# Weight halves of 4 bytes in turns in one tile, and every moving operand 128 bytes modulo 256 away

## The chip, the cores and the metric

The kernel runs on one core of one Trainium2 chip. The metric is the device time of one execution in microseconds. Five engines work side by side: TensorE (PE in the profile, its weight loads are PEld), VectorE (DVE), ScalarE (ACT), GpSimd (POOL) and SyncE (SP), which here only starts the DMAs.

## The reference

Two blocks of two layers each over 256 positions of width 1024, all in float32. Each layer is a mixer and a feed-forward net around a residual stream:

```python
x = x + ssd_mixer(rmsnorm(x), ...)        # state-space mixer, 32 heads
x = x + conv_ffn(rmsnorm(x), ...)         # up 1024 -> 5632, conv, silu(g)*u, down 2816 -> 1024
x = x + diff_attention(rmsnorm(x), ...)
x = x + conv_ffn(rmsnorm(x), ...)
# second block: four half-weighted swiglu nets of the same size, a conv mixer with
# attention to a memory, a forgetting attention with attention to a memory, a last rmsnorm
```

Nearly all of the arithmetic is in products of an activation (256 rows) with a weight matrix that is used once: 308.8 MB are read from HBM.

## The kernel before

**Three products for one.** TensorE takes float32 at full pace only as `F32R`, a float32 with fewer mantissa bits. So each operand is split into an upper part (rounded to `F32R`) and a lower part (the rest), and `mm3` adds three products: upper weight by upper activation (L212), upper weight by lower activation (L213), lower weight by upper activation (L214). Each of the three has a weight load of its own, which runs beside the matmul in front of it.

**Weights.** SP loads raw weights into `wr` (three buffers of 2048 floats). `split` takes 1024 columns of it (512 to 768 in some places): ScalarE writes the upper part to the tile `wh` (L202), VectorE subtracts it from the raw weights and writes the lower part to the tile `wl` (L206; in the first stage every fourth goes to GpSimd). Both tiles have five buffers of 4096 bytes a partition, so TensorE can be several pieces behind.

**Activations.** They stand transposed, 128 features by 256 positions, in tiles `xx` (a normed input, made by ScalarE L399 and VectorE L400), `gg` (a feed-forward's inner product) and `yy` (a mixer's output). In each, the upper part of a feature block is followed by its lower part, 1024 bytes each.

**Two forms of product.** In `lin_T` and `lin_out` (through `tile_T`, `tile_out` and `mm3`) 128 columns of the weights are the stationary operand and 256 columns of the activation move. `lin_T` makes projections with 8 blocks of features a tile; `lin_out` makes the eight tiles that go back to the residual stream. In `lin_N` (L285 to L287) it is the other way round: 128 positions of the activation are stationary and 512 columns of the weights move. It makes what is wanted untransposed: z of the state-space mixer (4 calls), query, key and value of the differential attention (6), the memory's values (2) and the forgetting attention's values (2), 14 calls of 48 matmuls each.

**Where the tiles lie.** `Net.t` rounds every tile's size up to `LINE` = 64 bytes. The pools follow each other in SBUF in the order in which they are opened. `wr`, `wh` and `wl` start at multiples of 256 bytes. Behind them L71 puts a tile "apart" of 64 bytes that nothing uses, so that all that follows is shifted by 64. In the built program the moving operands then start, modulo 256: `xx` at 64 in eleven cases and at 192 in three, `gg` at 192 in all six, `yy` at 64 in one and at 192 in three. Since every row of `xx`, `gg` and `yy` has 1024 bytes and every weight block 512, each matmul of a stage has the same distance modulo 256 between its moving operand and the weights that are loaded beside it.

**Order.** The code is written out in the order of the stages; `Net.spawn` and `adv` weave the small work of norms and attention heads into the stream of matmuls, and the tile framework sets the waits. A stage's stream is: load, split by ScalarE and VectorE, 24 matmuls for each split of 1024 columns.

Of the kernel before, what the change touches and what calls it, by code (L numbers as in the profile page):

```python
# [10 lines left out]
F32 = mybir.dt.float32  # L11
F32R = mybir.dt.float32r
# [11 lines left out]
LINE = 64  # L24
# [34 lines left out]
class Net:  # L59
    def __init__(self, ctx, tc, I, out):  # L60
        self.ctx, self.tc, self.nc, self.I, self.out = ctx, tc, tc.nc, I, out
        self.uid = 0
        nc = self.nc
        ps = bass.MemoryType.PSUM
        pool = lambda name, bufs, **k: ctx.enter_context(tc.tile_pool(name=name, bufs=bufs, **k))
        self.const = pool("const", 1)
        self.wr = pool("wr", 3)
        self.wh = pool("wh", 5)
        self.xp = pool("xp", 1)

        self.t(self.xp, [128, LINE // 4], F32, "apart")  # L71
        self.sm = pool("sm", 4)
        self.s2 = pool("s2", 2)
        self.psA = pool("psA", 3, space=ps)
        self.psM = pool("psM", 3, space=ps)
        self.psY = pool("psY", 2, space=ps)
        self.deferred = []
        self.hold = 1
        self.norm = None
        self.now = 0.0  # L80
        self.active = []
        self.waiting = []
        self.cnt = 0
        self.share = 0

        c = self.const
        self.X = self.t(c, [128, KD, S], F32, "X")
        self.cv = self.t(c, [128, NCOL], F32, "cv")
        self.mhalf = self.t(c, [128, 8], F32, "mhalf")
        nc.vector.memset(self.mhalf, -0.5)  # L90
        warm = self.t(c, [128, 8], F32, "warm")
        nc.scalar.activation(out=warm, in_=self.mhalf, func=AF.Silu)

        wz = self.t(self.s2, [128, S], F32, "dg").bitcast(BF16)
        nc.vector.memset(wz, 1.0)
        wp = self.psum(self.psM, "psM")
        for _ in range(11):
            nc.tensor.matmul(wp, lhsT=wz[:, 0:128], rhs=wz, start=True, stop=True)
        nc.sync.dma_start(out=self.cv[:, 0:8], in_=I["cv"][:, 0:8])
        self.first = self.t(self.wr, [128, 2048], F32, "wr")  # L100
        self.second = self.t(self.wr, [128, 2048], F32, "wr")
        for i in range(2):
            c0 = i * 512
            nc.sync.dma_start(out=self.first[:, c0:c0 + 512], in_=I["w_ssd"][0][:, c0:c0 + 512])
            for k in (4 * i, 4 * i + 2):
                nc.sync.dma_start(out=self.X[:, k:k + 2], in_=I["xT"][:, k:k + 2])
        for i in range(2):
            h = slice(i * 1024, i * 1024 + 1024)
            nc.sync.dma_start(out=self.second[:, h], in_=I["w_z"][0, 0][:, h])
        self.third = self.t(self.wr, [128, 2048], F32, "wr")  # L110
        nc.sync.dma_start(out=self.third, in_=I["w_z"][0, 1])
        nc.sync.dma_start(out=self.cv[:, 8:], in_=I["cv"][:, 8:])
        self.rv = self.t(c, [128, NROW], F32, "rv")
        nc.sync.dma_start(out=self.rv, in_=I["rv"].to_broadcast([128, NROW]))
        self.ident = self.t(c, [128, 128], F32, "ident")
        make_identity(nc, self.ident)
        self.identb = self.t(c, [128, 128], BF16, "identb")
        nc.vector.tensor_copy(out=self.identb, in_=self.ident)

        self.sel = self.t(c, [64, 32], F32R, "sel")  # L120
        for p in (0, 32):
            nc.vector.tensor_copy(out=self.sel[p:p + 32], in_=self.ident[p:p + 32, p:p + 32])
        self.ones = self.t(c, [128, 128], F32, "ones")
        nc.vector.memset(self.ones, 1.0)
        self.onesr = self.t(c, [128, 128], F32R, "onesr")
        nc.vector.tensor_copy(out=self.onesr, in_=self.ones)
# [70 lines left out]

    def split(self, raw, c0, n):
        nc = self.nc
        hi = self.t(self.wh, [128, 1024], F32R, "wh")  # L200
        lo = self.t(self.wh, [128, 1024], F32R, "wl")
        nc.scalar.activation(out=hi[:, :n], in_=raw[:, c0:c0 + n], func=AF.Copy)  # L202
        self.cnt += 1
        pool = self.share and self.cnt % self.share == 0 and (self.norm is None or self.norm.done)
        eng = nc.gpsimd if pool else nc.vector
        eng.tensor_tensor(out=lo[:, :n], in0=raw[:, c0:c0 + n],  # L206
                          in1=hi[:, :n].bitcast(F32), op=ALU.subtract)
        return hi, lo
# [120 lines left out]
    def make_norm(self, gname, split=True, sq="act", pool=None):  # L329
        return Norm(self, gname, split, sq, self.xp if pool is None else pool)  # L330
# [30 lines left out]
class Norm:  # L361
    def __init__(self, net, gname, split, sq, pool):
        self.n, self.g, self.split = net, gname, split
        self.done = False
        self.sq = sq
        self.keep = None
        self.wait = 4.5
        self.acc = net.t(net.s2, [128, S], F32, "nacc")
        if split:
            self.xx = net.t(pool, [128, KD, 2, S], F32R, "xx")  # L370
            self.xh, self.xl = self.xx[:, :, 0], self.xx[:, :, 1]
# [86 lines left out]
def first_norm(net, gname):  # L458
    nm = net.make_norm(gname)
    for k in range(KD):  # L460
        nm.scale(k, net.X[:, k])

    def squares():
        for k in range(KD):
            nm.add(k, net.X[:, k])
            if k % 2:
                yield 1

    nm.wait = 5.5
    net.spawn(squares(), 3)  # L470
    return nm


def next_norm(net, gname, split=True, pool=None):
    box = {}

    def after(m):
        if m == 0:
            box["n"] = net.make_norm(gname, split=split, pool=pool)
        box["n"].step(m)  # L480
    return box, after
# [866 lines left out]
def program(ctx, tc, I, out):  # L1348
    net = Net(ctx, tc, I, out)
    nc = net.nc  # L1350
    nm = first_norm(net, "nm0")
    box, after = next_norm(net, "nf0")
    ssd(net, nm, after)
    kvp = ctx.enter_context(tc.tile_pool(name="kvp", bufs=1))
    mk = net.t(kvp, [128, 4, S], F32, "mk")
    mv = net.t(kvp, [128, 2, 512], F32, "mv")
    tables = attn_tables(net, kvp)
    b2, after = next_norm(net, "nm1")
    ffn(net, box["n"], I["up0"], I["dn0"], 1.0, 0, after)
    b3, after = next_norm(net, "nf1")  # L1360
    diff_attn(net, b2["n"], mk, mv, kvp, tables, after)
    b4, after = next_norm(net, "f00")
    ffn(net, b3["n"], I["up1"], I["dn1"], 1.0, 1, after)
    b5, after = next_norm(net, "mx0")
    ffn(net, b4["n"], I["up2"], I["dn2"], 0.5, None, after)
    b6, after = next_norm(net, "f01")
    mixer_a(net, b5["n"], mk, mv, after)
    kvp = ctx.enter_context(tc.tile_pool(name="kvf", bufs=1))
    kT = net.t(kvp, [128, 8, S], F32, "kT")
    vN = net.t(kvp, [128, 2, D], F32, "vN")  # L1370
    cc2 = net.t(kvp, [64, S], F32R, "cc2")
    cN = net.t(kvp, [128, 2, 32], F32, "cN")
    cx = ExitStack()
    kvx = cx.enter_context(tc.tile_pool(name="kvx", bufs=1))
    b7, after = next_norm(net, "kvn", pool=kvx)
    ffn(net, b6["n"], I["up3"], I["dn3"], 0.5, None, after)
    n8 = kvf(net, b7["n"], "f10", kT, vN, cc2, cN)
    cx.close()
    b9, after = next_norm(net, "mx1")
    ffn(net, n8, I["up4"], I["dn4"], 0.5, None, after)  # L1380
    b10, after = next_norm(net, "f11")
    mixer_b(net, b9["n"], mk, mv, kT, vN, cc2, cN, after)
    b11, after = next_norm(net, "fin", split=False)
    fo = []

    def last(m):
        if m == 0:
            fo.append(net.t(net.xp, [128, 2 * KD, S], F32, "xx"))
        after(m)
        nc.scalar.activation(out=fo[0][:, m], in_=net.X[:, m], func=AF.Copy,  # L1390
                             scale=net.col("fin", m))

    ffn(net, b10["n"], I["up5"], I["dn5"], 0.5, None, last)
    fn = b11["n"]
    fn.force()
    fo = fo[0]
    for k in (0, 2, 1, 3, 4, 6, 5, 7):
        if k in (2, 6):
            nc.gpsimd.tensor_tensor(out=fo[:, k], in0=fo[:, k], in1=fn.R, op=ALU.mult)
        else:  # L1400
            nc.vector.tensor_tensor(out=fo[:, k], in0=fn.ps[:, :S], in1=fo[:, k], op=ALU.mult)
    for k in (0, 2, 4, 6):
        nc.sync.dma_start(out=out[:, k:k + 2], in_=fo[:, k:k + 2])
# [103 lines left out]
```

## Time and profile before

| what | value |
|---|---|
| time, median of 3 runs | 1809.99 us (1808.48 to 1810.47) |
| the profiled execution | 1804.52 us, of which the span of instructions is 1802.8 us |
| TensorE busy | 1768.8 us (98%) |
| VectorE, ScalarE, GpSimd busy | 1237.0 us (69%), 1016.0 us (56%), 490.2 us (27%) |
| granted clock of TensorE, mean | 0.995 |
| HBM traffic | 172 GB/s over the span |

A busy time is the sum of an engine's instructions. Matmuls are pipelined, so the bar of one (0.28 us) is longer than the distance to the next; the pace of TensorE is read from the distance of starts, or from how many bars touch a window of known length: (window + one bar) / count.

### The profile page before, as it was taken

To read this page: it belongs to the slowest core of one execution; us is meant where nothing else is said; L and a number is where in the kernel's file an instruction comes from. 1 tells how busy PE (TensorE), PEld (TensorE's weight loads), DVE (VectorE), ACT (ScalarE), POOL (GpSimd) and SP (SyncE) were. 2 spreads that over 40 slices of the span, in tenths; PEclk is the share of its full clock that TensorE was granted. 3 is DMA by queue.
4 is the path that set the end of the run, shared out by engine and by line. 5 is a ranking of instruction groups with operands and counts; after the bars stand their busy time and mean duration, and the time that the engine had idled before them with its cause. 6 is when DMAs were issued, how large, how long until landed. Compare 5 with 4: busy or idle time off the path is not lost.

```text
span 1802.8 us, 34773 instructions
## 1 busy us (share of the span) xinstructions
PE 1768.8 (98%) x14067; PEld 1702.7 (94%) x14067; DVE 1237.0 (69%) x1863; ACT 1016.0 (56%) x1661; POOL 490.2 (27%) x453
## 2 busy tenths in 40 slices
PE   8889999999999999999999999999999999999997
PEld 7787999998789999999999999999999998999997
DVE  6998789867786997655567775556655567575554
ACT  7666576656666765554455464455454455464443
POOL 3555224412211442133201214320033210024321
PEclk9999999999999999999999999999999999999999
DMA  6342645455326555655564475545555464265553
GB/s 234 117 141 71 210 169 194 164 178 189 137 89 229 180 188 158 212 187 187 162 216 161 140 235 181 186 155 193 210 187 187 154 221 164 73 231 180 187 161 106
DMA packets 76497, 312.12 MB, mean 173 GB/s; under 512 B 6192, under 2 KB 6320, under 8 KB 72624
## 3 DMA queue, kind: packets, MB, share of 16 engines
q1 hardware_dynamic: 76304, 309.89, 50.5%
q8 instruction: 111, 1.82, 0.4%
q14 instruction: 50, 0.41, 0.1%
q0 software_dynamic: 32, 0.00, 0.0%
HBM read 308.82 MB, written 1.05 MB: 172 GB/s over the span
## 4 chain that ended last, share of the span: by engine, by line
PE 87%; DVE 6%; ACT 2%; DMA 1%; POOL 1%; issue 1%; DVEq 0%; ACTq 0%; POOLq 0%
PE psA L214 25%; PE psA L213 25%; PE psA L212 25%; PE psA L285 2%; PE psA L287 2%; PE psA L286 2%; DVE cvy L848 2%; DVE wl L206 1%; POOL rs L342 1%; PE psM L992 1%; ACT wh L202 1%; DMA wr<-up 0%; PE psY L1137 0%; PE psM L1106 0%; DMA wr<-memT 0%
## 5 line engine op out<-in xcount | busy, mean ns | idle before, releaser
L206 DVE TENSOR_TENSOR wl<-wr,wh 128x1024 fp32r<-128x1024 f32 (+3 forms) x651 | 719.9, 1109 | 382.0 <-ACT wh L202 373.2
L202 ACT ACTIVATE wh<-wr 128x1024 fp32r<-128x1024 f32 (+3 forms) x660 | 629.2, 956 | 493.8 <-PE psA L213 312.4
L214 PE MATMUL psA<-xx,wl 128*128 128x256 f32 x2752 | 771.6, 280 | 4.6 <-DVE wl L206 4.6
L212 PE MATMUL psA<-xx,wh 128*128 128x256 f32 x2752 | 775.4, 282 | 0.4 <-DVE pad L352 0.4
L213 PE MATMUL psA<-xx,wh 128*128 128x256 f32 x2752 | 771.2, 280 | 0.0
L214 PEld LDWEIGHTS psA<-xx,wl 128*128 128x128 f32 x2752 | 517.4, 188 | 6.3 <-DVE wl L206 5.7
L212 PEld LDWEIGHTS psA<-xx,wh 128*128 128x128 f32 x2752 | 517.7, 188 | 2.1 <-PE psA L214 0.6
L213 PEld LDWEIGHTS psA<-xx,wh 128*128 128x128 f32 x2752 | 518.4, 188 | 0.9 <-issue 0.5
L213 PE MATMUL psA<-gg,wh 128*128 128x256 f32 x1056 | 294.1, 279 | 0.0
L214 PE MATMUL psA<-gg,wl 128*128 128x256 f32 x1056 | 294.1, 279 | 0.0
L212 PE MATMUL psA<-gg,wh 128*128 128x256 f32 x1056 | 294.1, 279 | 0.0
L503 POOL TENSOR_TENSOR p<-s,t 128x256 f32<-128x256 f32 x132 | 183.6, 1391 | 368.6 <-ACT s L531 368.6
L214 PEld LDWEIGHTS psA<-gg,wl 128*128 128x128 f32 x1056 | 200.5, 190 | 0.0
L213 PEld LDWEIGHTS psA<-gg,wh 128*128 128x128 f32 x1056 | 198.2, 188 | 0.0
L212 PEld LDWEIGHTS psA<-gg,wh 128*128 128x128 f32 x1056 | 198.2, 188 | 0.0
L390 POOL TENSOR_TENSOR nacc<-nacc,sq 128x256 f32<-128x256 f32 x72 | 63.6, 883 | 479.6 <-ACT sq L334 478.8
L506 POOL TENSOR_TENSOR gg<-p,gg 128x256 fp32r<-128x256 f32 x132 | 109.4, 830 | 125.7 <-ACT gg L505 125.7
L505 ACT ACTIVATE gg<-p 128x256 fp32r<-128x256 f32 x132 | 54.2, 412 | 126.7 <-POOL p L503 126.6
L212 PE MATMUL psA<-yy,wh 128*128 128x256 f32 x384 | 107.8, 282 | 0.2 <-ACT yy L1181 0.2
L213 PE MATMUL psA<-yy,wh 128*128 128x256 f32 x384 | 106.8, 279 | 0.3 <-DVE yy L1182 0.3
L214 PE MATMUL psA<-yy,wl 128*128 128x256 f32 x384 | 106.6, 278 | 0.0
L352 DVE TENSOR_TENSOR t<-psA,R 128x512 f32<-128x512 f32 (+1 forms) x104 | 69.3, 670 | 37.1 <-PE psA L214 35.5
(291 smaller groups left out, 1920.0 us busy)
## 6 DMA issues: line engine op xcount, KB each, us to landing
wr<-up SPq DMA_DIRECT2D x132, 1024.0 KB, 4.8
wr<-dn SPq DMA_DIRECT2D x96, 704.0 KB, 4.0
wr<-w_a SPq DMA_DIRECT2D x14, 1024.0 KB, 4.8
wr<-w_ssd SPq DMA_DIRECT2D x12, 1024.0 KB, 5.0
wr<-w_ain SPq DMA_DIRECT2D x12, 1024.0 KB, 4.8
wr<-w_ssdo SPq DMA_DIRECT2D x16, 512.0 KB, 4.5
wr<-w_z SPq DMA_DIRECT2D x7, 1024.0 KB, 4.8
wr<-w_ao SPq DMA_DIRECT2D x16, 384.0 KB, 3.1
```

What stands on the lines that cost most here:

```text
L202: nc.scalar.activation(out=hi[:, :n], in_=raw[:, c0:c0 + n], func=AF.Copy)
L206: eng.tensor_tensor(out=lo[:, :n], in0=raw[:, c0:c0 + n], in1=hi[:, :n].bitcast(F32), op=ALU.subtract)
L212: mm(ps, lhsT=wh, rhs=xh, start=first, stop=False)
L213: mm(ps, lhsT=wh, rhs=xl, start=False, stop=False)
L214: mm(ps, lhsT=wl, rhs=xh, start=False, stop=last)
L285: mm(ps[b], lhsT=xh[:, k, xs], rhs=hi[:, c], start=k == 0, stop=False)
L286: mm(ps[b], lhsT=xl[:, k, xs], rhs=hi[:, c], start=False, stop=False)
L352: self.nc.vector.tensor_tensor(out=o, in0=p, in1=self.bc(R, n), op=ALU.mult)
L390: eng.tensor_tensor(out=self.acc, in0=self.acc, in1=sq, op=ALU.add)
L503: nc.gpsimd.tensor_tensor(out=p, in0=s, in1=t[:, 1], op=ALU.mult)
L505: nc.scalar.activation(out=gh[:, j], in_=p, func=AF.Copy)
L506: nc.gpsimd.tensor_tensor(out=gl[:, j], in0=p, in1=gh[:, j].bitcast(F32), op=ALU.subtract)
```

## The change

Upper and lower weight parts now share one tile `w` of 128 x 1024 x 2 floats under the tag `wh`: the upper part is `w[:, :, 0]`, the lower `w[:, :, 1]`. ScalarE and VectorE write every second float, VectorE also reads the upper part with that step, weight loads of L212 to L214 read 128 floats at a step of 8 bytes (1024 bytes of address in place of 512), and in `lin_N` the moving operand is 512 floats at a step of 8 bytes. The unused tile behind the weights grows from 64 to 128 bytes, and a second one of 128 bytes stands at the start of the pool that holds the memory's keys and values. In the built program every `xx`, `gg` and `yy` then starts at 128 modulo 256 and every `wh` at 0. The buffers take as much room as before.

```diff
@@ Net.__init__
-        self.t(self.xp, [128, LINE // 4], F32, "apart")
+        self.t(self.xp, [128, 2 * LINE // 4], F32, "apart")
@@ Net.split
-        hi = self.t(self.wh, [128, 1024], F32R, "wh")
-        lo = self.t(self.wh, [128, 1024], F32R, "wl")
+
+        w = self.t(self.wh, [128, 1024, 2], F32R, "wh")
+        hi, lo = w[:, :, 0], w[:, :, 1]
@@ program
     kvp = ctx.enter_context(tc.tile_pool(name="kvp", bufs=1))
+    net.t(kvp, [128, 2 * LINE // 4], F32, "apart")
```

The order of instructions on each engine stays as it is but for some rows around attention heads that change places with a neighbour; lines below L200 count one more, those below L1356 two more. What differs along the stream is who waits. On VectorE, in a feed-forward's up projection of the second block, two loads of weights (four pieces) stood before as follows (`wl`, `wh`, `wr` with buffer numbers; L352 scales a finished product into `t`):

```order
L206 TENSOR_TENSOR wl_9294<-wr_9290,wh_9293 128x1024 [waits DMAHW7_49,Activation_49]
L206 TENSOR_TENSOR wl_9322<-wr_9290,wh_9321 128x1024 [waits PE_49,Activation_49]
L352 TENSOR_TENSOR t_9215<-psA_9158,R_9109 128x512 [waits PE_49,Pool_49]
L206 TENSOR_TENSOR wl_9361<-wr_9357,wh_9360 128x1024 [waits DMAHW0_49,Activation_49]
L206 TENSOR_TENSOR wl_9389<-wr_9357,wh_9388 128x1024 [waits PE_49,Activation_49]
L352 TENSOR_TENSOR t_9282<-psA_9225,R_9109 128x512 [waits PE_49,Pool_49]
```

The same place with the change:

```order
L207 TENSOR_TENSOR wh_9028<-wr_9025,wh_9028 128x1024 [waits DMAHW7_49,Activation_49]
L207 TENSOR_TENSOR wh_9055<-wr_9025,wh_9055 128x1024 [waits Activation_49]
L353 TENSOR_TENSOR t_8952<-psA_8897,R_8849 128x512 [waits PE_49,Pool_49]
L207 TENSOR_TENSOR wh_9093<-wr_9090,wh_9093 128x1024 [waits DMAHW0_49,Activation_49]
L207 TENSOR_TENSOR wh_9120<-wr_9090,wh_9120 128x1024 [waits Activation_49]
L353 TENSOR_TENSOR t_9017<-psA_8962,R_8849 128x512 [waits PE_49,Pool_49]
```

The subtraction no longer waits for TensorE itself: the buffer is one tile, and ScalarE, which writes it first, has waited for TensorE. TensorE's own waits are the same: L212 for ScalarE, L214 for VectorE.

## Rows read from the trace of the kernel before

**Rows 1.** The page: busy time by engine, and the chain by engine and line.
```profile
PE 1768.8 (98%) x14067; PEld 1702.7 (94%) x14067; DVE 1237.0 (69%) x1863; ACT 1016.0 (56%) x1661; POOL 490.2 (27%) x453
...
PE 87%; DVE 6%; ACT 2%; DMA 1%; POOL 1%; issue 1%; DVEq 0%; ACTq 0%; POOLq 0%
PE psA L214 25%; PE psA L213 25%; PE psA L212 25%; PE psA L285 2%; PE psA L287 2%; PE psA L286 2%; DVE cvy L848 2%; DVE wl L206 1%; POOL rs L342 1%; PE psM L992 1%; ACT wh L202 1%; DMA wr<-up 0%; PE psY L1137 0%; PE psM L1106 0%; DMA wr<-memT 0%
```

**Rows 2.** Groups by form: count, busy us, mean ns of one, idle before.
```profile
L214 PE MATMUL psA<-xx,wl 128*128 128x256 f32 x2752 | 771.6, 280 | 4.6 <-DVE wl L206 4.6
L213 PE MATMUL psA<-gg,wh 128*128 128x256 f32 x1056 | 294.1, 279 | 0.0
L212 PE MATMUL psA<-yy,wh 128*128 128x256 f32 x384 | 107.8, 282 | 0.2 <-ACT yy L1181 0.2
L285 PE MATMUL psA<-wh,xx 128*128 128x512 f32 x224 | 90.9, 406 | 0.0
```

**Rows 3.** TensorE's timeline and its weight loads', feed-forward of the second layer: start, length.
```profile
600.03 0.28 PE L212 MATMUL psA<-xx,wh 128*128 128x256 f32 x1
600.15 0.28 PE L213 MATMUL psA<-xx,wh 128*128 128x256 f32 x1
...
600.04 0.19 PEld L213 LDWEIGHTS psA<-xx,wh 128*128 128x128 f32 x1
```

**Rows 4.** Windows of TensorE inside single stages: length, busy us (bars), granted clock.
```profile
365.00:415.00 50.00, 50.00 (x427) 1.00 0.63 204
550.00:569.00 19.00, 19.00 (x171) 1.00 0.64 202
765.00:880.00 115.00, 115.00 (x979) 1.00 0.51 181
890.00:940.00 50.00, 50.00 (x444) 1.00 0.67 216
1040.00:1060.00 20.00, 20.00 (x179) 1.00 0.73 232
1195.00:1250.00 55.00, 55.00 (x470) 1.00 0.61 202
1430.00:1480.00 50.00, 50.00 (x443) 1.00 0.64 204
1580.00:1605.00 25.00, 25.00 (x215) 1.00 0.67 233
1735.00:1785.00 50.00, 50.00 (x444) 1.00 0.50 160
```

**Rows 5.** Timeline of TensorE at three places: runs of equal matmuls, start and whole length.
```profile
147.05 0.50 PE L774 MATMUL psY<-xdt,E 128*128 128x64 f32 x3
...
498.41 1.04 PE L972 MATMUL psM<-ident,qt 128*128 128x128 f32 x8
...
957.34 1.89 PE L1106 MATMUL psM<-mk,qmT 128*128 128x256 f32 x8
```

**Rows 6.** TensorE's timeline in a product of the second form, the forgetting attention's values.
```profile
1280.66 0.39 PE L285 MATMUL psA<-wh,xx 128*128 128x512 f32 x1
...
1283.40 0.39 PE L285 MATMUL psA<-wh,xx 128*128 128x512 f32 x1
```

**Rows 7.** Windows of all engines: length, then PE, PEld, DVE, ACT, POOL busy.
```profile
25.00:184.00 159.00, 145.51 (x963) 129.14 (x961) 141.98 (x243) 109.21 (x165) 76.93 (x49) 0.96 0.34 119
238.00:358.00 120.00, 119.58 (x1016) 119.41 (x1015) 109.29 (x169) 82.30 (x132) 50.17 (x42) 1.00 0.50 174
759.00:884.00 125.00, 125.00 (x1064) 125.00 (x1063) 69.12 (x75) 60.33 (x92) 45.19 (x43) 1.00 0.51 179
```

**Rows 8.** Groups by form: the two halves of a split, at 1024 and 512 columns.
```profile
L206 DVE TENSOR_TENSOR wl<-wr,wh 128x1024 fp32r<-128x1024 f32 x415 | 514.0, 1243 | 229.6 <-ACT wh L202 228.6
L202 ACT ACTIVATE wh<-wr 128x1024 fp32r<-128x1024 f32 x424 | 446.2, 1056 | 289.4 <-PE psA L213 151.3 <-issue 91.4 <-PE psA L286 21.1
L206 DVE TENSOR_TENSOR wl<-wr,wh 128x512 fp32r<-128x512 f32 x28 | 19.6, 701 | 20.7 <-ACT wh L202 20.4
L202 ACT ACTIVATE wh<-wr 128x512 fp32r<-128x512 f32 x28 | 17.6, 630 | 20.3 <-PE psA L286 6.6 <-PE psA L213 4.5 <-DMA wr<-w_aout 2.8
```

## The prediction

> **What bounds the kernel now.** I read the page first: TensorE is busy for 98% of the span, and the chain that ended last is TensorE for 87%, three quarters of it the three lines of `mm3` [rows 1]. The waits in front of these matmuls are a few microseconds in all [rows 2]. So the end is set by how fast TensorE goes through 12,576 matmuls of 256 columns (three times 2752 + 1056 + 384) [rows 2], and the next question is their pace.
>
> The timeline shows it: L212 starts at 600.03 and L213 at 600.15, and the weight load for L213 starts together with L212's matmul, at 600.04 [rows 3]. Matmul and next load run side by side, both reading SBUF. The windows give the pace exactly, as (window + 0.28) / bars: 50.28/427 = 117.8 ns, 115.28/979 = 117.8 and 55.28/470 = 117.6 in three stages, but 50.28/444 = 113.2 in two, 50.28/443 = 113.5, 20.28/179 = 113.3 and 19.28/171 = 112.8 in others [rows 4]. [...]
>
> What could the floor be? [...] L774 moves 64 columns, so only its weight load can hold it: three bars of 0.27 in 0.50, that is 0.112 apart; a load alone needs 112 ns [rows 5]. Transposes (L972) take (1.04 - 0.27)/7 = 110 ns with a load each [rows 5]. [...]
>
> I compared this with the starting addresses of the tiles. The long stages whose moving operand starts at 64 modulo 256, all six up projections, run at 117.8 (765 is the start of such a window). Those at 192 run at 113.3 (down projections of the third, fifth and sixth net, 890, 1430 and 1735; two out projections, 550 and 1040) or at 117.8 (down projections of the first, second and fourth net, 365 and 1195 among them; the last out projection, 1580), each for its whole length [rows 4]. So the loss depends on where the two streams stand to each other, and on the phase in which a stage falls in. That is a collision of two readers in SBUF.
>
> [...]
>
> **The change part by part.** *Step of 8 bytes in weight loads.* Now a load goes through 512 bytes of address while the matmul goes through 1024, so one stream overtakes the other and their distance runs through all values modulo 256. With the step of 8, both go through 1024 bytes in about the same time, and start together [rows 3]; with 128 modulo 256 at the start they stay half a period apart. If the collision has a period of 256 or less, it should vanish, or be gone after the first stall. The price of a step then is bounded as follows. [...] Above: if a load needs twice its time for twice the address range, about 214, +96 ns on 12,576 = +1.2 ms. The matmul itself already reads 1024 bytes in 113 ns at the best pace seen [rows 4], the same rate of address as the new load, so I take the load as unharmed: 112 ns, the load's own row [rows 5].
>
> The sum: 2,064 matmuls run at 113.3 now (three down projections of 8 x 22 x 3 = 528, out projections of 192 and 288). Of the other 10,512, 576 are the state-space projections (4 groups of 6 tiles, 24 matmuls each), where VectorE is busy 142 of 159 us and TensorE waits for it [rows 7]: nothing is gained there. That leaves 9,936 x (117.8 - 112) = 57.6 us, and 2,064 x 1.3 = 2.7 us. At the seen 113.3 it would be 9,936 x 4.5 = 45 us; at 109, 9,936 x 8.8 + 2,064 x 4.3 = 96 us.
>
> What is late next: in the two nets with a convolution VectorE is busy 109.3 of 120 us [rows 7]; a whole up projection is 1,056 x 117.8 = 124.4 us, so about 113, and TensorE would need 118.3. It still leads, by little; I take 1 us off for each, -2 us. In the other nets VectorE has 69 of 125 [rows 7].
>
> *Step of 8 bytes on ScalarE and VectorE.* No row shows such a step there. Both halves run at one pace per element: (1243 - 701)/512 = 1.06 ns on VectorE, (1056 - 630)/512 = 0.83 on ScalarE [rows 8]. Below: no gain, since the pace per element stays. Above: two beats per element, +1.08 and +0.85 us per 1024. In a net without convolution 44 pieces, +47 us, would end at 69 + 47 = 116 of 118 us, still hidden; in the two with convolution 113 + 47 = 160, +42 us each; in the state-space part some 32 pieces, +35 us: up to +120 us. I take 0, the pace of the rows.
>
> *Step of 8 bytes in the moving operand of `lin_N`.* 672 matmuls of 512 columns, at 228 ns. [...] Above: two beats a column as in L1106, 2 x 216 = 431, +203 x 672 = +136 us. The full-pace stream has to go through 2048 bytes of address more per step than any row shows. I take 0: nearest is the same instruction with a step of 4. [...]
>
> *One tile in place of two.* ScalarE's write now waits until the lower part of the buffer's old content is used, one matmul (0.12 us) later, with five buffers in hand; VectorE drops its wait for TensorE. TensorE's waits stay. Cost 0: all of VectorE's idle time before the subtraction is already for ScalarE (229 us) [rows 8]. If that cover went, it is 0.12 us for each piece at which TensorE has run dry, a few in the whole kernel.
>
> *Alignment.* The unused tiles cost nothing but room. [...]
>
> Sum: -57.6 - 2.7 + 2 = -58 us. The profiled execution took 1804.5 us (span 1802.8 and 1.7 around it) and would take 1746; the median of the runs is 5.5 us above it, so I set the forecast from that: 1810 - 58 = 1752 us.
>
> **The rivals.** *The second form slows.* In `lin_N` a moving column at a step of 8 takes two beats; first-form stages gain as above. 1810 - 58 + 136 = 1888. [...] Against: nothing shows a limit in bytes. It decides once a `lin_N` matmul gains 58/672 = 86 ns, from 314 ns on.
>
> *Loads collide more.* A load touches twice as many stretches of SBUF, and each costs the same beats as now, in spite of the offset: the excess over 112 doubles to 123.6 and 114.6, 9,936 x 5.8 + 2,064 x 1.3 = +60, 1870. For it: the loss is already there with half the stretches, and no stage shows a distance of 128. Against: it is smaller at one offset than at the other, so place matters.
>
> [...]
>
> *Writers too slow*, two beats on VectorE: 1752 to 1872, by the figures above.
>
> **How the numbers follow.** Forecast 0.50, own range 1714 (all at 109) to 1780 (113.3, with some of `lin_N` or VectorE lost). A gain mostly eaten, 1780 to 1806: 0.09. Nothing happens, 1806 to 1814 (0.2% is what runs of this kernel can tell): 0.10. Slower: loads collide more 0.13, `lin_N` 0.12, writers 0.06. So faster 0.59, same 0.10, slower 0.31. The range of 8 in 10 leaves out little below 1712, and above 1865 the most part of the `lin_N` case and half of the collision case.
>
> **What would show it.** Right: windows in FFN stages at (window + 0.28)/bars near 112, equal in all stages; L202 and L206 at 1056 and 1243 ns; `lin_N` at 216 to 230. [...]

## The result, and the profile after

The changed kernel takes 1993.84 us (median of 3 runs, 1991.91 to 1997.48), 1.102 times the time before (95% interval 1.0994 to 1.1048). It is slower by 184 us; the forecast was 1752 us with a range that ended at 1865.

The page of the changed kernel (busy time by engine; then the chain that ended last, by engine and by line):

```profile
PE 1972.2 (99%) x14067; PEld 1777.3 (89%) x14067; DVE 1243.1 (62%) x1863; ACT 1067.8 (54%) x1661; POOL 495.2 (25%) x453
...
PE 92%; DVE 3%; DMA 1%; issue 1%; POOL 1%; ACT 1%; SPq 0%; DVEq 0%; ACTq 0%; POOLq 0%
PE psA L213 24%; PE psA L214 24%; PE psA L215 24%; PE psA L286 5%; PE psA L288 5%; PE psA L287 5%; DVE cvy L849 1%; DVE wh L207 1%; PE psM L993 1%; DMA wr<-w_ssd 0%; PE psY L775 0%; ACT wh L203 0%; PE psY L1138 0%; PE psM L1107 0%; DMA wr<-up 0%
```

Against [rows 1] the order of things has not changed: TensorE is the bound, for 92% of the chain now. But its share in `lin_N` (L286 to L288) went from 6% to 15%. So no new wait came in; TensorE's own work became longer, in the first form (`mm3`) and most of all in the second (`lin_N`).

Groups by form of the changed kernel (count, busy us, mean ns of one, idle time before and what ended it), against [rows 2, 8]:

```profile
L215 PE MATMUL psA<-xx,wh 128*128 128x256 f32 x2752 | 783.1, 285 | 2.4 <-DVE wh L207 2.4
...
L207 DVE TENSOR_TENSOR wh<-wr,wh 128x1024 fp32r<-128x1024 f32 x415 | 514.9, 1243 | 356.3 <-ACT wh L203 355.5
L203 ACT ACTIVATE wh<-wr 128x1024 fp32r<-128x1024 f32 x424 | 488.7, 1155 | 380.9 <-PE psA L215 153.0 <-PE psA L288 108.3 <-issue 101.3
...
L286 PE MATMUL psA<-wh,xx 128*128 128x512 f32 x224 | 143.9, 643 | 0.0
...
L207 DVE TENSOR_TENSOR wh<-wr,wh 128x512 fp32r<-128x512 f32 x28 | 20.0, 716 | 39.3 <-ACT wh L203 39.0
...
L203 ACT ACTIVATE wh<-wr 128x512 fp32r<-128x512 f32 x28 | 18.9, 676 | 31.3 <-PE psA L288 16.1 <-PE psA L215 5.4 <-DMA wr<-w_aout 5.1
```

The bar of a `lin_N` matmul grew from 406 to 643 ns. ScalarE's strided write takes 1155 ns where it took 1056 (9% more), VectorE's takes the same 1243. TensorE waits for neither (2.4 us before L215), and both idle more than before; what ScalarE mostly waits for is TensorE, which frees the buffers.

Windows inside single stages of the changed kernel (length, PE, PEld, DVE, ACT, POOL busy, granted clock, DMA share, GB/s), against [rows 4]:

```profile
405.00:455.00 50.00, 50.00 (x415) 50.00 (x414) 29.66 (x37) 26.63 (x39) 4.92 (x7) 1.00 0.60 194
825.00:880.00 55.00, 55.00 (x456) 55.00 (x455) 33.45 (x43) 29.19 (x44) 6.72 (x8) 1.00 0.59 194
1210.00:1330.00 120.00, 120.00 (x992) 119.93 (x992) 65.90 (x68) 62.95 (x89) 45.08 (x42) 1.00 0.52 174
...
1470.00:1590.00 120.00, 120.00 (x993) 120.00 (x993) 64.41 (x64) 61.57 (x84) 43.90 (x40) 1.00 0.51 170
```

(Window + one bar)/count gives 50.29/415 = 121.2, 55.29/456 = 121.2, 120.29/992 = 121.3 and 120.29/993 = 121.1 ns. The two paces of before, 113.3 and 117.8, are gone, and so far the prediction was right: one pace everywhere. But it is 121, not 112, at the same granted clock of 1.00.

TensorE's timeline in a product of the second form of the changed kernel, the forgetting attention's values (start, length), against [rows 6]:

```profile
1423.63 0.63 PE L288 MATMUL psA<-wh,xx 128*128 128x512 f32 x1
1424.08 0.63 PE L286 MATMUL psA<-wh,xx 128*128 128x512 f32 x1
...
1439.04 0.63 PE L286 MATMUL psA<-wh,xx 128*128 128x512 f32 x1
```

Between the first and the last of these rows lie 34 steps: 15.41/34 = 453 ns for 512 columns, where it was (1283.40 - 1280.66)/12 = 228.

**The account.** I took the distances of starts over the whole of both traces, between neighbours without a wait. First form: 117.00 ns before, 121.05 after, +4.05 x 12,576 = +51 us. `lin_N`: 231.9 before, 453.1 after, +221 x 672 = +149 us. The sum is +200; the spans of the profiled executions differ by 1995.8 - 1802.8 = +193 us. The other 7 us I put down to waits that a slower TensorE hides: by the two pages TensorE is idle for 1802.8 - 1768.8 = 34.0 us before and for 1995.8 - 1972.2 = 23.6 us after, and VectorE's share of the chain fell from 6% to 3%. No run singles out which waits went.

### The profile page after: what moved, and what is told of

It reads as the page before. It is cut to its first block, busy times and chain, and to the rows that moved or that the text cites. A ratio compares the mean times of both kernels' runs of the same rounds, so it can differ in the third digit from the quotient of the medians.

```text
span 1995.8 us, 34571 instructions
## 1 busy us (share of the span) xinstructions
PE 1972.2 (99%) x14067; PEld 1777.3 (89%) x14067; DVE 1243.1 (62%) x1863; ACT 1067.8 (54%) x1661; POOL 495.2 (25%) x453
## 4 chain that ended last, share of the span: by engine, by line
PE 92%; DVE 3%; DMA 1%; issue 1%; POOL 1%; ACT 1%; SPq 0%; DVEq 0%; ACTq 0%; POOLq 0%
PE psA L213 24%; PE psA L214 24%; PE psA L215 24%; PE psA L286 5%; PE psA L288 5%; PE psA L287 5%; DVE cvy L849 1%; DVE wh L207 1%; PE psM L993 1%; DMA wr<-w_ssd 0%; PE psY L775 0%; ACT wh L203 0%; PE psY L1138 0%; PE psM L1107 0%; DMA wr<-up 0%
## 5 line engine op out<-in xcount | busy, mean ns | idle before, releaser
L207 DVE TENSOR_TENSOR wh<-wr,wh 128x1024 fp32r<-128x1024 f32 (+3 forms) x651 | 724.6, 1114 | 551.0 <-ACT wh L203 549.7
L203 ACT ACTIVATE wh<-wr 128x1024 fp32r<-128x1024 f32 (+3 forms) x660 | 686.3, 1042 | 605.1 <-PE psA L215 323.7
L213 PE MATMUL psA<-xx,wh 128*128 128x256 f32 x2752 | 793.9, 288 | 0.5 <-ACT wh L203 0.3
L214 PE MATMUL psA<-xx,wh 128*128 128x256 f32 x2752 | 786.6, 286 | 0.0
L215 PE MATMUL psA<-xx,wh 128*128 128x256 f32 x2752 | 783.1, 285 | 2.4 <-DVE wh L207 2.4
L215 PEld LDWEIGHTS psA<-xx,wh 128*128 128x128 f32 x2752 | 542.7, 197 | 3.4 <-DVE wh L207 3.1
L214 PEld LDWEIGHTS psA<-xx,wh 128*128 128x128 f32 x2752 | 542.0, 197 | 1.3 <-issue 0.9
L213 PEld LDWEIGHTS psA<-xx,wh 128*128 128x128 f32 x2752 | 538.5, 196 | 3.4 <-issue 0.7
L213 PE MATMUL psA<-gg,wh 128*128 128x256 f32 x1056 | 301.2, 285 | 0.0
L214 PE MATMUL psA<-gg,wh 128*128 128x256 f32 x1056 | 300.9, 285 | 0.0
L215 PE MATMUL psA<-gg,wh 128*128 128x256 f32 x1056 | 298.5, 283 | 0.0
L215 PEld LDWEIGHTS psA<-gg,wh 128*128 128x128 f32 x1056 | 207.6, 197 | 0.0
L214 PEld LDWEIGHTS psA<-gg,wh 128*128 128x128 f32 x1056 | 207.1, 196 | 0.0
L213 PEld LDWEIGHTS psA<-gg,wh 128*128 128x128 f32 x1056 | 205.0, 194 | 0.0
L286 PE MATMUL psA<-wh,xx 128*128 128x512 f32 x224 | 143.9, 643 | 0.0
L287 PE MATMUL psA<-wh,xx 128*128 128x512 f32 x224 | 143.1, 639 | 0.0
L288 PE MATMUL psA<-wh,xx 128*128 128x512 f32 x224 | 143.0, 641 | 0.0
L214 PE MATMUL psA<-yy,wh 128*128 128x256 f32 x384 | 109.7, 286 | 0.0
```

The source lines that it names most:

```text
L207: eng.tensor_tensor(out=lo[:, :n], in0=raw[:, c0:c0 + n], in1=hi[:, :n].bitcast(F32), op=ALU.subtract)
L213: mm(ps, lhsT=wh, rhs=xh, start=first, stop=False)
L214: mm(ps, lhsT=wh, rhs=xl, start=False, stop=False)
L215: mm(ps, lhsT=wl, rhs=xh, start=False, stop=last)
L286: mm(ps[b], lhsT=xh[:, k, xs], rhs=hi[:, c], start=k == 0, stop=False)
L287: mm(ps[b], lhsT=xl[:, k, xs], rhs=hi[:, c], start=False, stop=False)
```

## The experiments

**Each part alone.** All on the kernel before. The theory at this point: `lin_N` at a step of 8 and first-form loads at a step of 8 each cost TensorE by themselves, and the shift to 128 is a third, smaller term. The rivals: the two costs come from the new distance, or one of them from the other.

`e1_step`, the tile in turns, unused tiles as before:

```diff
-        hi = self.t(self.wh, [128, 1024], F32R, "wh")
-        lo = self.t(self.wh, [128, 1024], F32R, "wl")
+        w = self.t(self.wh, [128, 1024, 2], F32R, "wh")
+        hi, lo = w[:, :, 0], w[:, :, 1]
```

> The change's first part alone: halves in turns, offsets 64 and 192 as before. Theory (the step costs by itself): lin_N matmuls about 450 ns and first-form matmuls 119 to 123, time 1975 to 2010 us. Rival (the offset of 128 is what hurts): lin_N near 232, first form 113 to 118, time 1790 to 1830 us.

`e2_apart`, the shift alone, halves contiguous:

```diff
-        self.t(self.xp, [128, LINE // 4], F32, "apart")
+        self.t(self.xp, [128, 2 * LINE // 4], F32, "apart")
...
+    net.t(kvp, [128, 2 * LINE // 4], F32, "apart")
```

> The change's second part alone: halves in two tiles as before, all moving operands at 128 modulo 256. Theory (the step costs by itself): lin_N near 230, first form 113 to 118, time 1770 to 1825 us. Rival (the offset of 128 is what hurts): first form 120 ns or more, time 1850 us or more.

`e3_mixed`, the whole change but for `lin_N`, whose halves are contiguous (`turns=False`):

```diff
+        w = self.t(self.wh, [128, 2048], F32R, "wh")
+        if turns:
+            w = w.rearrange("p (c t) -> p c t", t=2)
+            hi, lo = w[:, :, 0], w[:, :, 1]
+        else:
+            hi, lo = w[:, :1024], w[:, 1024:]
```

> The change, but where weights move (lin_N) the halves stand one behind the other in the tile, not in turns. Theory (two beats for a moving column at a step of 8): 672 x 222 ns = 149 us come back, 1835 to 1855 us, first form unchanged at 117 to 126. Rival (lin_N is slow for another reason, the shared tile or the offset): 1960 us or more.

`e7_second`, the opposite: only `lin_N` in turns, unused tiles as before.

> Only the products of the second form (lin_N) get their weights in turns, 512 moving columns at a step of 8 bytes; all other splits keep contiguous halves in one tile, and the unused tiles are as before. Theory: these 672 matmuls go from 232 to 453 ns, +149 us, the rest keeps its paces of 113.3 and 117.8 ns: 1805 + 149 = 1954 us, give or take 8. Rival: part of what lin_N costs in the changed kernel comes from the distance of 128 or from first-form stages beside it, and the cost is not additive: then the time lies under 1940 or over 1970 us.

| kernel | time, us | ratio to before (95%) | first form, ns | `lin_N`, ns |
|---|---|---|---|---|
| before | 1805.0 | | 117.0 | 232 |
| `e1_step` | 1981.5 | 1.0978 (1.0959 to 1.0996) | 120.2 | 453 |
| `e2_apart` | 1827.7 | 1.0125 (1.0107 to 1.0142) | 119.1 | 232 |
| `e3_mixed` | 1859.6 | 1.0301 (1.0285 to 1.0316) | 121.0 | 233 |
| `e7_second` | 1950.3 | 1.0792 (1.0759 to 1.0825) | 117.5 | 453 |

So `lin_N` at a step of 8 costs 145 us alone (`e7_second`) and the rest of the change 55 us (`e3_mixed`); together 200, where the whole change costs 184 to 189 against the two medians of before. Within 16 us the parts add up: neither cost comes from the other. `e1_step` and `e7_second` came in as expected. `e2_apart` and `e3_mixed` ended 3 and 5 us above their theory's ranges, and far from their rivals in time; `e2_apart`'s pace, 119.1 ns, lies between the theory's 118 and the rival's 120. So the shift contributes a loss, not a gain, on the halves as they were: `e2_apart` is slower by 23 us with nothing but another distance. Its windows (columns as above):

```profile
362.00:412.00 50.00, 50.00 (x423) 50.00 (x423) 30.39 (x39) 25.44 (x39) 4.57 (x6) 1.00 0.63 202
...
1080.00:1195.00 115.00, 115.00 (x961) 115.00 (x960) 64.62 (x66) 57.61 (x85) 43.58 (x41) 1.00 0.51 175
```

50.28/423 = 118.9 and 115.28/961 = 120.0 ns: both of its paces are worse than either pace of before. `e7_second` has the single tile too, and its first form stays at 117.5 ns (117.0 before): "one tile in place of two" costs nothing that shows.

**The operations by themselves.** Four maps leave the net out: rows of equal matmuls, each with a weight load of its own, on idle engines.

`m1_map` varies the step of either operand and the distance, in steps of 32 bytes:

```python
for gap in (32, 48):
    for w in (flatw, turnw):              # loads at a step of 4, of 8 bytes
        for off in range(0, 256, 32):     # distance of the moving operand
            first_form(w, off, gap)       # 96 matmuls of 256 columns, then one short one
```

> This kernel leaves the whole net out: it only runs short rows of 96 (or 48) F32R matmuls back to back, so its time means nothing and only the distances of starts count. Theory (step of 8 is dear, place is second): 512 moving columns 216 to 235 ns apart at a step of 4 bytes and about 450 at 8, with or without changing weights; loads beside 64 moving columns 112 ns at every step; 256 columns beside loads at a step of 4 bytes 113 to 118 at all offsets of 0 to 224, beside loads at a step of 8 some 118 to 125 at all offsets. Rival (place decides): at a step of 8 one or more offsets give 112 or less and others 125 or more, with the best not at 128.

The timeline of `m1_map` (start, length of the whole row of equal matmuls): 48 matmuls of 512 moving columns at a step of 4, 8 and 16 bytes, all with the same block of weights (which is loaded again before each), then rows of 96 with loads at a step of 4 at distances 0 and 64, at a step of 8 at 0, and at a step of 16:

```profile
142.90 11.15 PE L74 MATMUL acc<-mov,wflat 128*128 128x512 f32 x48
...
153.92 22.01 PE L74 MATMUL acc<-mov,wflat 128*128 128x512 f32 x48
...
175.80 22.37 PE L74 MATMUL acc<-mov,wflat 128*128 128x512 f32 x48
...
198.03 11.76 PE L61 MATMUL acc<-mov,wflat 128*128 128x256 f32 x96
...
220.98 11.13 PE L61 MATMUL acc<-mov,wflat 128*128 128x256 f32 x96
...
288.95 11.77 PE L61 MATMUL acc<-mov,wturn 128*128 128x256 f32 x96
...
566.50 22.66 PE L61 MATMUL acc<-mov,wfour 128*128 128x256 f32 x96
```

The first three rows settle `lin_N`: by the distances of starts 227, 453 and 461 ns for 512 columns. A step of 8 halves the pace of the moving stream, a step of 16 adds next to nothing, and with other weights before each matmul it is the same (227, 453, 461). The layout of the net and the step of the loads have no part in it: these loads are contiguous. Every matmul here has a load, so a stream without one was not measured; but at a step of 8 a load runs for less than half of each matmul's 453 ns (bars of 0.21 us, then 0.24 to 0.25 us without one; in the window 155 to 174 the loads are busy for 8.67 of 19.00 us), and the same loads leave the stream at a step of 4 at 227 ns. That the stream does it by itself is therefore likely, not shown. The other rows: about 120 and 113 ns at a step of 4 (distances 0 and 64), 120 at a step of 8, 233 at a step of 16. At a step of 8 all eight distances gave 120 to 122 ns; at a step of 4 they gave 113.3 (64 and 192), 116.7 to 118.6 (32, 128, 160, 224) and 120 (0, 96). So the expected 113 to 118 for loads at a step of 4 did not hold at 0 and 96; the loads at a step of 8 lose at all of these distances, and 128 is not a good one even for contiguous halves. Rows in which 64 columns moved ran at half the clock (granted 0.50) in this map, so a load's own time stayed open.

`m2_map` takes it at the full clock, by nine such matmuls behind 24 full ones, and repeats distances 64 and 192 with weights in another place and with other gaps.

> The net is left out again: short rows of matmuls, of which only the distances of starts count. (a) Nine loads beside 64 moving columns, between full-pace rows that keep the clock at its upper level. Theory (a load at a step of 8 is no longer by itself; it is dear only beside a full-pace stream): 112 ns at steps of 4 and 8, more at 16. Rival (the load itself takes longer at 8): about 120 at 8. (b) 256 moving columns at a step of 8: theory (a column at a step of 8 takes two beats) 220 to 230 ns whatever the load does. (c) Distances of 64 and 192 with weights at 0 and at 128 modulo 256, after four kinds of start: theory (two phases of one layout) 113.3 or 117.8 in whole rows, both paces at the same distance; rival (the place alone decides) one pace for each place. (d) Distances at multiples of 16 between those of the first map: 113 to 121.

Nine loads at a step of 4, 8 and 16 in the timeline of `m2_map`, each followed by the short matmul that ends the row:

```profile
42.21 1.17 PE L91 MATMUL acc<-mov,wflat 128*128 128x64 f32 x9
43.22 0.26 PE L57 MATMUL sep<-mov,wflat 128*128 128x32 f32 x1
...
54.37 1.23 PE L91 MATMUL acc<-mov,wturn 128*128 128x64 f32 x9
55.44 0.26 PE L57 MATMUL sep<-mov,wflat 128*128 128x32 f32 x1
...
66.71 2.27 PE L91 MATMUL acc<-mov,wfour 128*128 128x64 f32 x9
68.82 0.26 PE L57 MATMUL sep<-mov,wflat 128*128 128x32 f32 x1
```

From start to start over nine: 1.01/9 = 112, 1.07/9 = 119, 2.11/9 = 234 ns. My theory expected 112 for the step of 8 as well: a miss. The load at a step of 8 is 7 ns longer when only 64 columns move beside it.

The traces of the net confirm it with next to nothing beside the load. In nine places the first load of a first-form product follows matmuls of one column (L409 before, L410 in the changed kernel). In the kernel before the loads there follow one another at 111 to 112 ns, the figure of L774's row [rows 5]: from its start to the start of the next load is a load's own time. One of the nine places in the kernel before, then the same one in the changed kernel, with the matmuls of one column at the end:

```profile
237.55 0.19 PEld L212 LDWEIGHTS psA<-xx,wh 128*128 128x128 f32 x1
237.66 0.19 PEld L213 LDWEIGHTS psA<-xx,wh 128*128 128x128 f32 x1
...
276.30 0.20 PEld L213 LDWEIGHTS psA<-xx,wh 128*128 128x128 f32 x1
276.42 0.20 PEld L214 LDWEIGHTS psA<-xx,wh 128*128 128x128 f32 x1
...
275.96 0.50 PE L410 MATMUL psM<-ones,nacc 128*128 128x1 f32 x4
276.33 0.38 PE L213 MATMUL psA<-xx,wh 128*128 128x256 f32 x1
```

In whole nanoseconds the distance is 111 or 112 in all nine places before, 119 or 120 in all nine of the changed kernel, and 118 to 120 in `e1_step`, `e3_mixed` and (below) `e10_turn112`; in `e2_apart`, where only the layout changed, it is 111 or 112. So the load at a step of 8 takes 7 to 8 ns more by itself, and that is the larger part of what the first form lost against the forecast of 112.

Of the other parts of `m2_map`, 256 moving columns at a step of 8 took 231 ns with loads at a step of 4 and 230 with loads at 8, as expected. The repeated rows at 64 and 192 were each at 113.3 or 117.8 as a whole. At 192 the same place gave either (weights at 128: two of six rows at 113.3; weights at 0: four of four); at 64 all rows of this map were at 117.8, where `m1_map` had 113.3 twice. So the two paces are two phases of one layout. Between the points of the first map 112 alone was fast, 113.9 ns against 116.7 to 120.

`m3b_map` puts matmuls of random length between rows of 48, so that each starts in another phase: eight rows for each distance at a step of 4, four at a step of 8.

> The net is left out again; only the distances of starts count. Rows of 48 matmuls of 256 columns, each after a random number of matmuls of random width, eight times at each distance of 0, 32, ... 224 with weights at a step of 4 bytes, four times at a step of 8. Theory (a load at a step of 8 meets the stream too often for any place): at a step of 8 no row under 119 ns, at any distance, after any start; at a step of 4 two paces at 64 and 192, 113.3 and 117.8, in proportions that the place sets only in part. Rival (the place decides, and the earlier maps saw one phase only): some rows at a step of 8, above all at 128, at 112 or less.

Loads at a step of 8: 119.9 to 122.8 ns in all 32 rows. At a step of 4: a distance of 192 gave about 113.6 in six rows of eight, 64 in one of eight (113.3, otherwise 117.7 to 119.6), every other distance 116.6 or more. No phase brings the step of 8 down.

`m4_map` has every multiple of 8 bytes, both steps, two rows each; it was run last, after `e9_d112` (below) had shown that the grid of 32 was too coarse.

> The net left out. Rows of 48 matmuls of 256 columns with a load each, at every distance that is a multiple of 8 bytes, twice, with matmuls of random length between the rows: loads at a step of 4 and at a step of 8. Theory: step 8 stays at 120 ns or more at all 32 distances; step 4 is at 113.3 in both rows at 112 and a few distances near it. Rival: step 8 too has distances with 113 ns or less, only not at multiples of 32, and the prediction's idea of two streams in lockstep failed by the choice of 128 alone.

The timeline of `m4_map`: a row at a step of 8 (`wturn`) at a distance of 80, at a step of 4 and of 8 at 88, and at a step of 4 at 112:

```profile
542.48 5.82 PE L98 MATMUL acc<-mov,wturn 128*128 128x256 f32 x48
...
548.33 5.92 PE L98 MATMUL acc<-mov,wflat 128*128 128x256 f32 x48
...
554.14 6.13 PE L98 MATMUL acc<-mov,wturn 128*128 128x256 f32 x48
...
584.63 5.64 PE L98 MATMUL acc<-mov,wflat 128*128 128x256 f32 x48
```

(Row - 0.28)/47: 117.9, 120.0, 124.5 and 114.0 ns. The first is the lowest of the 64 rows at a step of 8 (117.8 by the starts); the highest is 125. At a step of 4 only 192 (113.6 and 113.9) and 112 (116.3, and 114.2 in the last row shown) come under 116.5; odd multiples of 8 give 118 to 124. The rival, a distance at which the step of 8 runs at 113 or less, is not there. My theory missed too, by less: eight of the 32 distances have a row at a step of 8 between 117.8 and 119.9, and 112 at a step of 4 is not at 113.3 in these rows.

**Other distances, halves contiguous.** `e4_all192` and `e5_all64` bring all moving operands to 192 or to 64 with weights at 0, by unused tiles of other sizes:

```diff
-        self.t(self.xp, [128, LINE // 4], F32, "apart")
+        self.t(self.xp, [128, 3 * LINE // 4], F32, "apart")
...
+    net.t(kvp, [128, 2 * LINE // 4], F32, "apart")
```

(`e5_all64` has only the last line of it.)

> Halves in two tiles as before, all moving operands at 192 modulo 256 (before: most at 64). Theory (64 holds the slow phase in this kernel, 192 allows the fast one): many of the 10,200 matmuls at 117.8 go to 113.3, 1765 to 1795 us. Rival (phase alone, place without effect between 64 and 192): 1800 to 1812 us.

> Halves in two tiles as before, all moving operands at 64 modulo 256. Theory (64 holds the slow phase): the 2,100 matmuls at 113.3 go to 117.8, +9 us, 1810 to 1817 us. Rival (phase alone): some stages at 113.3 still, 1795 to 1810 us.

`e6_w128` and `e8_w128m64` move the weights to 128 by one more unused tile, with the moving operands at 192 and at 64:

```diff
+        self.gap = pool("gap", 1)
+        self.t(self.gap, [128, 2 * LINE // 4], F32, "gap")
         self.wh = pool("wh", 5)
```

> Contiguous halves as before, but all weight buffers at 128 and all moving operands at 192 modulo 256. Two places in the map of shuffled starts gave 113.6 ns in 6 of 8 rows at this pair, against 31% of the first form at 113.3 in the kernel with weights at 0. If the pair decides, about three quarters of 12,400 matmuls run at 113.3: some 1790 us. Rival: the phase decides and the pair is as good as the one with weights at 0: 1800 to 1808 us, no difference from before.

> Contiguous halves as before, weights at 128 and all moving operands at 64 modulo 256, a distance of 192. The expectation for e6_w128 misread its row of the map: the 6 of 8 rows at 113.6 ns were this pair, while weights at 128 and moving operands at 192 are a distance of 64, with 1 row of 8. Theory: only the distance counts, and at 192 the kernel runs as with weights at 0 and moving operands at 192: 1788 to 1812 us, median some 1803. Rival: this pair itself holds 113.3 in three quarters of the first form: some 1775 us.

`e9_d112` is `e5_all64` with the data of `xx`, `gg` and `yy` 48 bytes into a longer tile:

```diff
+        if tag in ("xx", "gg", "yy") and dt == F32R:
+            v = pool.tile([128, n + 64], dt, tag=tag, name=name)[:, 12:12 + n]
+            return v.rearrange("p (a b c) -> p a b c", b=shape[2], c=shape[3])
```

> Contiguous halves as before, weights at 0 and all moving operands at 112 modulo 256. The second map had one row of 96 matmuls at this distance, at 113.3 ns. Theory: as with 64 and 192 this is the better of two phases of one layout, and the kernel falls into both: 1788 to 1815 us, no clear difference. Rival: at 112 the pace is 113.3 in every phase: 1805 - 10,200 x 4.5 ns = 1759 us.

`e10_turn112` adds to it the turns of `e3_mixed` (first form alone).

> As e9_d112 (moving operands at 112 modulo 256, lin_N with contiguous halves), but the first form's weights in turns at a step of 8 bytes. Theory: the first form goes from 113.3 to 120 or 121 ns, 12,600 x 7 = +88 us on 1765: 1853 us, as e3_mixed at a distance of 128. Rival: at 112 the step of 8 costs nothing: 1760 to 1770 us.

| kernel | distance (weights, moving) | time, us | ratio to before (95%) | first form, ns |
|---|---|---|---|---|
| `e4_all192` | 192 (0, 192) | 1802.9 | 0.9984 (0.9956 to 1.0013) | 116.4 |
| `e8_w128m64` | 192 (128, 64) | 1791.2 | 0.9936 (0.9919 to 0.9952) | 115.7 |
| `e5_all64` | 64 (0, 64) | 1811.5 | 1.0034 (1.0015 to 1.0052) | 117.7 |
| `e6_w128` | 64 (128, 192) | 1812.8 | 1.0030 (1.0013 to 1.0046) | 117.7 |
| `e9_d112` | 112 (0, 112) | 1764.9 | 0.9785 (0.9769 to 0.9801) | 113.6 |
| `e10_turn112` | 112, step of 8 | 1853.0 | 1.0245 (1.0200 to 1.0289) | 120.0 |

At 64 both kernels agree, wherever the weights stand, and nearly all of the first form is at the worse pace (some 98% of the matmuls near 117.8 in both). At 192 a share is at the better one, much of it by whole stages: 31% in `e4_all192`, 47% in `e8_w128m64`. So the distance counts, and at 192 the phase. Whether the place of the weights also has a part in the phase is open: the two kernels at 192 differ by 12 us, and their intervals do not meet. The theory of `e4_all192` (1765 to 1795 us) missed; that of `e5_all64` held; `e8_w128m64` came out inside its theory's range, but between the expected median of 1803 and the rival's 1775. `e6_w128` was chosen by a misread row of the map, as the next expectation says, so its forecast of 1790 us fell; it served as the second kernel at 64 instead.

`e9_d112` beats both kernels: 1764.9 us, 2.2% under before and 11.5% under the changed one. Its windows:

```profile
355.00:405.00 50.00, 50.00 (x444) 50.00 (x443) 31.74 (x41) 27.22 (x43) 5.60 (x8) 1.00 0.64 209
565.00:680.00 115.00, 114.57 (x1009) 114.35 (x1008) 108.29 (x156) 82.54 (x131) 49.39 (x41) 1.00 0.55 197
747.00:860.00 113.00, 113.00 (x998) 113.00 (x997) 65.38 (x69) 57.72 (x86) 44.54 (x42) 1.00 0.53 186
...
1695.00:1745.00 50.00, 50.00 (x443) 50.00 (x443) 26.91 (x34) 25.64 (x40) 6.04 (x7) 1.00 0.50 160
```

50.28/444 = 113.2, 113.28/998 = 113.5: every long feed-forward stage has the good pace, the up projections too that stood at 117.8. In the second window VectorE is busy 108 of 115 us and TensorE waits 0.4 us: the cover that the prediction saw as thin there holds at this pace. My theory had expected two phases here too (1788 to 1815); it was the rival's 1759 that came near. `e10_turn112` then put the step of 8 at this very distance: +88 us, as expected. That it is right to the microsecond is luck: the expected 7 ns a matmul were 6.4, which is 80 us, and the four runs spread from 1845 to 1856. So the step is slow by itself, as the load's own 118 to 120 ns say, and no distance that I tried saves it.

## Why the prediction was wrong

**The step that failed first is "Step of 8 bytes in weight loads".** It said that two streams that go through addresses at the same rate and start half a period apart stay apart, so that the collision "should vanish", at 112 ns. The streams do get one pace, in all stages, but it is 121. The term that was mis-sized is the load taken "as unharmed: 112 ns": by itself it takes 118 to 120 ns, with one column beside it in the net and with 64 in `m2_map`, and in no phase and at none of 32 distances does the first form run under 117.8. The upper bound of its price was a slip: twice 112 is 224 ns, not 214. No run shows the 109 ns on which the lower end of the range, 1714 us, rests: the lowest pace of the first form over a stage was 112.8 to 113.6 ns ([rows 4], `e9_d112`). Beyond the load's own time the changed kernel loses 1 to 2 ns, contiguous halves at the same distance 7 (119.1 against 112). So the idea that the collision shrinks with two streams in step is not refuted by these runs; what failed is the price of the load that it needed. The price of the load came from a row of the old form (L774 [rows 5]); the argument that the matmul reads addresses at the same rate in 113 ns carried that price over from one reader to another. The forecast of -58 us became +51. The second rival, "loads collide more", had 1870 us; `e3_mixed`, which has the slower first form alone, took 1859.6. That is near by luck: the mechanism that the rival told (more stretches, the same excess for each) would have kept two paces of 123.6 and 114.6, and there is one of 121.

**The larger error is the 0 for `lin_N`.** The prediction bounded it by twice L1106's 216 ns, 431 ns or +136 us, and took 0 because the nearest row was the same instruction at a step of 4. Measured: 453 ns, +149 us. The bound was right in size and slightly short, since it rested on another stream, (1.89 - 0.38)/7 = 216 ns for 256 columns of plain float32 [rows 5]; twice the 227 of the same stream at a step of 4 is 454. Nor does a run show the 216 that opens the span for "right", 216 to 230: 512 `F32R` columns with a load each took 227 ns at the least (`m1_map`). A row with the old step is no row for the new one: nothing in the trace spoke for 0 against twice the time, and 0.12 for this rival was too little.

**Two rivals' outcomes came together, and no case held both.** A slower first form (+60 by the second rival's price) and `lin_N` (+136) add to 2006 us; the measurement is 1994. They touch different matmuls and do not exclude each other, as `e3_mixed` and `e7_second` show. Treated as exclusive, their range ended at 1865. With chances of their own, both together had to have a place above 1900.

**What held.** TensorE's pace sets the end, and with contiguous halves its loss is a matter of where the two streams stand: by the layout alone, with the same instructions, the first form went from 113.6 (`e9_d112`) to 119.1 ns (`e2_apart`), 63 us apart. This decides against "nothing happens", the outcome of 0.10 in which the layout is worth nothing. VectorE at a step of 8 costs nothing at 1024 columns (1243 ns in both kernels), ScalarE 9% (1155 ns against 1056), far below the +1.08 and +0.85 us feared, and both are hidden (TensorE is idle for 2.4 us before L215). One tile costs nothing that shows (`e7_second`, 117.5 ns against 117.0).

**What stays open.** Why a distance of 112 is fast in the net (113.6 ns) and less so in `m4_map` (114.2 and 116.3), why 192 is so only in one phase, what sets the phase, why a load at a step of 8 takes 7 to 8 ns more by itself, whether a moving stream at a step of 8 is as slow without any load, and whether what the two streams lose to each other is a collision of readers in SBUF, as the prediction has it. The runs show that it is so, not by which mechanism.

## What to carry to other kernels

Before an operand of a full-pace engine gets another step, measure that operand with that step in a row by itself: a row of the old step says nothing about it, and here the moving operand lost half its pace (227 to 453 ns) and the load 7% (112 to 119 or 120). Mechanisms that touch different instructions need a case in which they all happen, in the sum and in the range. Where two reads run side by side, scan their distance in fine steps: the winner (112) lay between the points of a grid of 32 and was worth 2.2%. A map only points to it: whether a distance is good was settled by the whole kernel.

## What the runs showed of the hardware

- A moving `F32R` operand of 512 columns, a contiguous weight load beside it: 227 ns at a step of 4 bytes, 453 at 8, 461 at 16 (`m1_map`).
- A weight load at full clock beside 64 moving columns: 112 ns at a step of 4, 119 at 8, 234 at 16 (`m2_map`); beside one column 111 to 112 at a step of 4 and 118 to 120 at 8 (the kernels). Matmuls of 256 columns with a load each: 113 to 124 ns by distance at a step of 4, 117.8 to 125 at 8, 233 or more at 16 (the maps).
- Matmuls of 256 columns with a load each, in the kernel before: `F32R` 113 to 118 ns [rows 4], plain float32 216 (L1106) [rows 5].
- One layout can have two paces, each for a whole stage: at a distance of 192, 113.2 in the window at 890 and 117.8 in the one at 365 [rows 4]. That a kernel falls into them differently from run to run would explain why ten runs of `e4_all192` spread from 1788 to 1812 us and four of `e9_d112` only from 1764 to 1768; one run of each was traced, so it isn't shown.
- A write at a step of 8 bytes: ScalarE 1155 ns against 1056 for 1024 columns, VectorE 1243 against 1243.
